# Where the stacked halves of the next attention head are copied on ScalarE: free to float, or tied behind exponentials of the current head

## The chip, the cores and the metric

The kernel runs on one core of one Trainium2 chip. A core has a matrix engine (TensorE, PE in the profile), a vector engine (VectorE, DVE), an engine for activations and copies (ScalarE, ACT), a general one (GpSimd, POOL) and DMA queues (SP issues most of them). Each engine works through its own list of instructions in order; semaphores make an instruction wait for another engine's. The metric is the device time of one execution in microseconds. Three runs of the kernel before gave 1568.66 to 1571.03 us, the median is 1570.81 us.

## What is computed

Two transformer layers over 512 image tokens and 256 context tokens, width 1024. The first layer ("even") has a gated MLP branch and a differential attention; the change touches only that attention:

```python
def diff_attn(q, k, v, lam):
    s = jnp.einsum('bqhd,bkhd->bhqk', q, k).astype(jnp.float32) * ATTN_SCALE
    p = jax.nn.softmax(s, axis=-1).reshape(b, B_HEADS, 2, tq, tk)
    a = p[:, :, 0] - lam * p[:, :, 1]
    return jnp.einsum('bhqk,bkhe->bqhe', a.astype(v.dtype), v)
```

There are four heads (B_HEADS), and each has two halves of 64 channels. Each half has a softmax of its own, and the second is subtracted from the first with the weight lam. The 512 image queries see all 768 keys, the 256 context queries only the 256 context keys.

## The kernel before

The four heads run one after the other: `head(t)` calls `attend` for three pairs of query blocks (qp 0 and 1 are image queries, qp 2 the context queries). A pair has four softmax pieces (two blocks of 128 queries, two halves c).

One softmax piece is a chain over three engines (`softmax_diff`, L534 to L545). TensorE multiplies queries and keys into a PSUM tile `pw` (L535, L536; 768 columns for image queries, 256 for context ones). There are only two such tiles, so a third piece waits until the exponential of the first has read its tile. VectorE takes the row maximum (L537), ScalarE the exponential into `e` (L539), and VectorE combines two of them (L543 to L545). Then `attend` transposes `e` on TensorE into a `pb` bank (L558); ScalarE casts the bank to `ath` and VectorE takes the rest `atl` (L131, L132); TensorE multiplies both with the values (L115 to L117, tiles `pb`), and ScalarE copies the sum into `o` (L570).

Queries and keys go in as "stacks". A product in full precision is split into a rounded part and a remainder, and 64 channels of each fill the 128 rows of the matrix engine. `stack(t, c)` (L587 to L598) builds it for half c of head t. ScalarE makes three copies of 64x768: keys into `kh` (L593), queries into `qs` (L594), keys again into the other rows of `kh` (L595). VectorE makes two subtractions of 64x768 (L596 into `qs`, L597 into `kl`). `kh` and `qs` have three buffers each: two hold the current head, one is free. So the first half of the next head can be copied as soon as its inputs are there, and the second half not before half 0 of the current head has made its last product.

`attend(t, ..., qp)` calls `stack(t + 1, 0)` at qp 1 and `stack(t + 1, 1)` at qp 2. The order of each engine's list is not the order of the code: a scheduler sets it from priorities and its own costs. `head(t)` runs at a raised priority, and ahead of it stands work that has nothing to do with the heads and can fill TensorE: `block` (projections of q and k for heads 2 and 3) and `gated` (the MLP branch). Their products are the `pf` tiles. There is one `pf` buffer, so after each of them ScalarE must copy it out (L442, L579) before the next can start. `issue_after(x)` adds an order, not a wait on another engine: what stands in its block comes behind x in the list of x's own engine.

Of the kernel before, what the change touches and what calls it, by code (L numbers as in the profile page):

```python
# [27 lines left out]
class Builder:  # L28
# [291 lines left out]
    def even(self):  # L320
        tc, nc, a = self.tc, self.nc, self.a
# [15 lines left out]
        for k in range(0, KT, 2):  # L337
            t = self.load(Rh, a["xT"][k * P:(k + 2) * P, :].rearrange("(k p) t -> p k t", p=P), [P, 2, TX], f"hx{k}")
# [111 lines left out]
        for k in range(KT):  # L450
            t = self.adap.tile([P, 2, 512], F32R, name=self.uid("wq"), tag="wq", bufs=2) if k in (2, 5) else None
# [8 lines left out]
            t, sh = hx[k], self.modcol(0, 0, k, 0)  # L460
# [31 lines left out]
        for k in range(KT):  # L492
            W = self.unit(a["v0"][k * P:(k + 1) * P, :], 512)
            for tb in range(6):
                c = slice(tb * P, (tb + 1) * P)
# [28 lines left out]
        def softmax_diff(Q, K, qb, sums):  # L524


            koff = 0 if qb < 4 else TX
            qs = slice(qb * P, (qb + 1) * P)
            nm, sums = self.small(2, "sa", 10), sums[:, 2 * qb:2 * qb + 2]
            es = []  # L530
            for c in range(2):
                ps = self.wide()
                for p in range(2):
                    if qb < 4:  # L534
                        nc.tensor.matmul(ps[:, :TX], Q[c][:, qs], K[c][p][:, :TX], start=p == 0, stop=p == 1)  # L535
                    nc.tensor.matmul(ps[:, TX:TA], Q[c][:, qs], K[c][p][:, TX:], start=p == 0, stop=p == 1)  # L536
                nc.vector.tensor_reduce(nm[:, c:c + 1], ps[:, koff:TA], axis=AX, op=ALU.max, negate=True)  # L537
                e = Ra.tile([P, TA], F32, name=self.uid("e"), tag="e", bufs=6)
                self.last_exp = nc.scalar.activation(e[:, koff:], ps[:, koff:TA], AF.Exp, bias=nm[:, c:c + 1],  # L539
                                                     accum_out=sums[:, c:c + 1])  # L540
                es.append(e[:, koff:])
            r = self.small(1, "sa", 10)
            nc.vector.reciprocal(r, sums[:, 1:2])  # L543
            nc.vector.scalar_tensor_tensor(r, r, self.nlam, sums[:, 0:1], ALU.mult, ALU.mult)
            nc.vector.scalar_tensor_tensor(es[0], es[1], r, es[0], ALU.mult, ALU.add)  # L545
            return es[0]

        def attend(t, Q, K, qp, o, eps):
            es = [softmax_diff(Q, K, 2 * qp + i, eps) for i in range(2)]
            if qp and t < 3:  # L550
                stack(t + 1, qp - 1)
            kbs = list(range(6)) if qp < 2 else [4, 5]
            po = self.bank()[:, :TC]
            for i in range(0, len(kbs), 2):
                pt = self.bank()
                for j in range(2):
                    for b in range(2):
                        nc.tensor.transpose(pt[:, j * TC + b * P:j * TC + (b + 1) * P],  # L558
                                            es[b][:, (i + j) * P:(i + j + 1) * P], self.ident)
                th = Ra.tile([P, 512], F32R, name=self.uid("ath"), tag="at", bufs=6)  # L560
                tl = Ra.tile([P, 512], F32R, name=self.uid("atl"), tag="at", bufs=6)
                self.split(th, tl, pt)
                for j in range(2):
                    kb = kbs[i + j]
                    c = slice(t * P, (t + 1) * P)
                    m = slice(j * TC, (j + 1) * TC)
                    self.mm3(po, (vhi[kb][:, c], vlo[kb][:, c]), (th[:, m], tl[:, m]),
                             i + j == 0, i + j == len(kbs) - 1)
            s = slice(qp * TC, (qp + 1) * TC)
            nc.scalar.copy(o[:, s], po)  # L570
# [13 lines left out]
            nc.gpsimd.memset(lows[i][0][64:128].bitcast(F32), 0.0)  # L584
            nc.gpsimd.memset(lows[i][1][0:64].bitcast(F32), 0.0)

        def stack(t, c):  # L587

            q, k, low = qk[t], qk[4 + t], lows[t % 2][c]
            X, Y = (slice(0, 64), slice(64, 128))[::1 - 2 * c]  # L590
            qs = Ra.tile([P, TA], F32R, name=self.uid("qs"), tag="sq", bufs=3)
            kh = Ra.tile([P, TA], F32R, name=self.uid("kh"), tag="kh", bufs=3)
            nc.scalar.copy(kh[X], k[X])  # L593
            nc.scalar.copy(qs[X], q[X])  # L594
            nc.scalar.copy(kh[Y], k[X])  # L595
            nc.vector.tensor_tensor(qs[Y], q[X], qs[X].bitcast(F32), ALU.subtract)  # L596
            nc.vector.tensor_tensor(low[X], k[X], kh[X].bitcast(F32), ALU.subtract)  # L597
            QK.setdefault(t, []).append((qs, (kh, low)))  # L598
# [51 lines left out]
        def head(t):  # L650
            Q, K = zip(*QK[t])
            o = f3("o", 4)
            eps = self.small(12, "sx", 2)
            for qp in range(3):
                attend(t, Q, K, qp, o, eps)
                if qp == 0:
                    norm(t - 1, 1)
                elif qp == 1:
                    norm(t - 1, 2)
            norms[t] = o, eps  # L660
            norm(t, 0)
            if t == 3:
                norm(t, 1)
                norm(t, 2)
            oraw.append(o)
# [50 lines left out]
        for c in range(2):  # L716
            stack(0, c)
# [42 lines left out]
        for k in order:  # L760
# [9 lines left out]
            elif k == 6:  # L770
                after = self.last_hi
# [1106 lines left out]
```

## Time and profile before

| | us |
|---|---|
| median of three runs (1568.66, 1570.81, 1571.03) | 1570.81 |
| the profiled execution, its own time | 1569.63 |
| its span | 1567.8 |
| the four heads, about | 165 to 325 |
| TensorE busy in that stretch of 160 us | 148.28 |
| VectorE busy in it | 126.38 |
| ScalarE busy in it | 98.21 |

The span runs from the first to the last instruction that the profiler saw; the time of the same execution is 1.8 us longer. "Busy" of TensorE is the time in which a matmul is in the pipeline. A row of the view of the order of time gives the start, the length, the engine, the line and, in brackets, how long the engine had been idle before and what released it.

### The profile page before, as it was taken

What the parts mean: (1) busy time and instruction counts of PE and PEld (TensorE: products, weight loads), DVE (VectorE), ACT (ScalarE), POOL (GpSimd) and SP (SyncE); (2) the same over time, 40 slices, a digit from 0 to 9 for tenths busy, and PEclk for the clock granted to TensorE, in tenths of its full rate; (3) what the DMA queues carried; (4) which work ended last, traced back from release to release, by engine and by line L of the source; (5) the groups of instructions that cost most, each with busy time, mean ns of one, the idle gap of its engine ahead of it and who ended that gap; (6) DMA issues with size and microseconds to landing.
All of it is one profiled execution on the core that took longest, in us unless ns stands there. A gap on an engine that the chain in (4) does not pass through costs nothing.

```text
span 1567.8 us, 24952 instructions
## 1 busy us (share of the span) xinstructions
PE 1513.8 (97%) x9563; PEld 1355.0 (86%) x9563; DVE 1069.2 (68%) x1890; ACT 726.4 (46%) x1489; POOL 820.0 (52%) x558
## 2 busy tenths in 40 slices
PE   6999999999999999999999999999999999999998
PEld 4767888889999999999999988777869889999997
DVE  3612777875688787888786487765657966666665
ACT  2415666563552333333333254555656544444444
POOL 0453322041256776777776454531304389888882
PEclk9999999999999999999999999999999999999999
DMA  9762100052123333454542212110224132323201
GB/s 350 298 243 74 45 21 1 1 192 77 68 76 120 114 114 116 141 160 144 168 166 70 79 55 65 57 32 16 65 106 162 55 118 91 113 90 114 89 21 55
DMA packets 53416, 162.27 MB, mean 104 GB/s; under 512 B 6192, under 2 KB 8624, under 8 KB 45616
## 3 DMA queue, kind: packets, MB, share of 16 engines
q1 hardware_dynamic: 46240, 135.37, 25.4%
q10 hardware_dynamic: 7056, 25.30, 4.9%
q8 instruction: 75, 1.23, 0.3%
q14 instruction: 45, 0.37, 0.1%
HBM read 158.55 MB, written 2.10 MB: 102 GB/s over the span
## 4 chain that ended last, share of the span: by engine, by line
PE 85%; DVE 9%; ACT 3%; issue 2%; DMA 1%; POOL 0%; DVEq 0%; SPq 0%; ACTq 0%; POOLq 0%
PE pw L116 11%; PE pw L115 11%; PE pw L117 11%; PE pb L116 9%; PE pb L115 9%; PE pb L117 9%; PE pf L115 4%; PE pf L116 4%; PE pf L117 4%; PE pb L1688 2%; PE pb L1677 2%; PE pf L359 2%; PE pw L1639 1%; PE pw L1647 1%; DVE t L49 1%
## 5 line engine op out<-in xcount | busy, mean ns | idle before, releaser
L836 DVE SCALAR_TENSOR_TENSOR xT<-pb,mod,xT 128x512 f32<-128x512 f32 (+3 forms) x204 | 143.2, 708 | 129.4 <-PE pb L117 128.9
L116 PE MATMUL pw<-ax,w 128*128 128x384 f32 (+2 forms) x716 | 227.6, 318 | 3.5 <-DVE ax L49 2.2
L115 PE MATMUL pw<-ax,w 128*128 128x384 f32 (+2 forms) x716 | 226.1, 319 | 3.6 <-DVE q L49 1.9
L117 PE MATMUL pw<-ax,w 128*128 128x384 f32 (+2 forms) x716 | 227.3, 318 | 0.1
L92 POOL TENSOR_TENSOR w<-raw,w 128x512 fp32r<-128x512 f32 (+1 forms) x76 | 111.9, 1478 | 202.0 <-ACT w L89 193.1
L49 POOL TENSOR_TENSOR w<-raw,w 128x512 fp32r<-128x512 f32 x122 | 185.1, 1533 | 48.5 <-ACT w L49 48.3
L49 POOL TENSOR_TENSOR w<-t,w 128x512 fp32r<-128x512 f32 x99 | 149.7, 1515 | 55.6 <-ACT w L49 55.6
L115 PE MATMUL pb<-hh,w 128*128 128x512 f32 x480 | 171.2, 357 | 1.2 <-DVE xT L836 1.2
L117 PE MATMUL pb<-hh,w 128*128 128x512 f32 x480 | 171.6, 357 | 0.4 <-DVE w L49 0.4
L116 PE MATMUL pb<-hh,w 128*128 128x512 f32 x480 | 171.3, 357 | 0.0
L115 PE MATMUL pw<-T,w 128*128 128x384 f32 (+1 forms) x508 | 156.6, 310 | 2.5 <-DVE hs L1044 1.2
L116 PE MATMUL pw<-T,w 128*128 128x384 f32 (+1 forms) x508 | 157.0, 310 | 1.2 <-DVE T L132 1.2
L117 PE MATMUL pw<-T,w 128*128 128x384 f32 (+1 forms) x508 | 157.0, 310 | 0.0
L115 PE MATMUL pf<-ax,w 128*128 128x256 f32 (+2 forms) x460 | 151.4, 329 | 2.1 <-DVE qf L264 1.4
L117 PE MATMUL pf<-ax,w 128*128 128x256 f32 (+2 forms) x460 | 149.3, 325 | 0.0
L116 PE MATMUL pf<-ax,w 128*128 128x256 f32 (+2 forms) x460 | 149.1, 324 | 0.0
L116 PEld LDWEIGHTS pw<-ax,w 128*128 128x128 f32 x716 | 136.4, 190 | 8.8 <-DVE ax L49 2.7
L115 PEld LDWEIGHTS pw<-ax,w 128*128 128x128 f32 x716 | 135.6, 190 | 8.0 <-DVE q L49 2.7
L117 PEld LDWEIGHTS pw<-ax,w 128*128 128x128 f32 x716 | 136.4, 190 | 2.3 <-DVE w L1007 0.4
L49 POOL TENSOR_TENSOR hh<-hs,hh 128x768 fp32r<-128x768 f32 (+1 forms) x42 | 77.3, 1839 | 95.0 <-ACT hh L49 70.9
L49 POOL TENSOR_TENSOR w<-rawo,w 128x512 fp32r<-128x512 f32 x59 | 103.6, 1756 | 28.2 <-ACT w L49 28.2
L240 DVE SCALAR_TENSOR_TENSOR junk<-ar,cb 128x1024 bf16<-128x1024 f32 x64 | 106.7, 1667 | 0.0
(417 smaller groups left out, 3909.7 us busy)
## 6 DMA issues: line engine op xcount, KB each, us to landing
raw<-ffn_in SPq DMA_DIRECT2D x44, 1024.0 KB, 5.1
ar<-ada SPq DMA_DIRECT2D x24, 1024.0 KB, 6.8
ar<-ada ACTq DMA_DIRECT2D x48, 512.0 KB, 3.6
rawo<-ffn_out SPq DMA_DIRECT2D x88, 256.0 KB, 3.0
raw<-odd_out SPq DMA_DIRECT2D x28, 256.0 KB, 2.6
raw<-qk SPq DMA_DIRECT2D x16, 256.0 KB, 4.6
raw<-uv SPq DMA_DIRECT2D x16, 256.0 KB, 2.9
raw<-even_out SPq DMA_DIRECT2D x8, 512.0 KB, 3.6
```

What stands on the lines that cost most here:

```text
L49: self.tail[key] = fn(*args, **kw)
L92: eng.tensor_tensor(lo, raw, hi.bitcast(F32), ALU.subtract)
L115: mm(out, s[0], m[0], start=start, stop=False, **kw)
L116: mm(out, s[0], m[1], start=False, stop=False, **kw)
L117: return mm(out, s[1], m[0], start=False, stop=stop, **kw)
L240: return self.nc.vector.scalar_tensor_tensor(junk, t, 1.0, self.cb[who], ALU.mult, ALU.mult, accum_out=self.acc[who][:, col:col + 1])
L359: nc.tensor.matmul(ps[32 * q:32 * q + 32, :w], cst[:, k, :], t[:, w * q:w * q + w], start=k == 0, stop=k == KT - 1, skip_group_check=True)
L836: ins = self.nc.vector.scalar_tensor_tensor(h, ps[:, r], self.modcol(l, j, m, who), h, ALU.mult, ALU.add)
L1639: nc.tensor.matmul(ps[:, st:en], Q, K[g][p][:, b0 * P:b1 * P], start=p == 0, stop=p == 1, skip_group_check=True)
L1647: last = nc.tensor.matmul(ps[:, en:en + TC], Q, K[g][p][:, TX:], start=p == 0 and not edge, stop=p == 1, skip_group_check=True)
L1677: last = nc.tensor.transpose(pt[:, x * P:(x + 1) * P], es[2 * (x % 2) + x // 2][:, kb * P:(kb + 1) * P], self.ident)
L1688: nc.tensor.matmul(po[64 * h:64 * h + 64, :], V[vb][:, 64 * g:64 * g + 64], t[:, h * TC:h * TC + TC], start=kb == 0, stop=kb == nb - 1, sk ...
```

## The change

`softmax_diff` already keeps its latest exponential in `self.last_exp`. Now `attend` also keeps the last one of qp 0 as `self.first_exps`, and `stack` gets an instruction behind which its three ScalarE copies are placed: `first_exps` for half 0 of the next head, the last exponential of qp 2 for half 1. The two VectorE subtractions are not tied. The stacks of head 0 are called without it. Nothing is added to what is computed.

```diff
         def attend(t, Q, K, qp, o, eps):
             es = [softmax_diff(Q, K, 2 * qp + i, eps) for i in range(2)]
+            if qp == 0:
+                self.first_exps = self.last_exp
             if qp and t < 3:
-                stack(t + 1, qp - 1)
+                stack(t + 1, qp - 1, self.last_exp if qp == 2 else self.first_exps)
...
-        def stack(t, c):
+        def stack(t, c, after=None):
...
-            nc.scalar.copy(kh[X], k[X])
-            nc.scalar.copy(qs[X], q[X])
-            nc.scalar.copy(kh[Y], k[X])
+            with tc.issue_after(after.ins) if after else ExitStack():
+                nc.scalar.copy(kh[X], k[X])
+                nc.scalar.copy(qs[X], q[X])
+                nc.scalar.copy(kh[Y], k[X])
```

The built programs differ in the order of all engines but the DMA queue, within the stretch of the heads. Lines behind the change are 1 to 3 higher in the new kernel. In the names below, `kh_1856` and `qs_1855` are half 1 of head 1, `kh_2177` and `qs_2176` half 0 of head 2; `e_1832` to `e_1849` are the context exponentials of head 0 (qp 2).

**ScalarE, from head 0 to head 1.** Before:

```order
L539 ACTIVATE e_1832,sx_1635<-pw_1828,sa_1821 128x256
L131 CAST ath_1699<-pb_1694 128x512
L593 CAST kh_1856<-f_58_332 64x768
L595 CAST kh_1856<-f_58_332 64x768
L131 CAST ath_1714<-pb_1709 128x512
L594 CAST qs_1855<-f_57_331 64x768
L593 CAST kh_2177<-f_219_1576 64x768
L595 CAST kh_2177<-f_219_1576 64x768
L594 CAST qs_2176<-f_211_1508 64x768
L539 ACTIVATE e_1843,sx_1635<-pw_1839,sa_1838 128x256
L539 ACTIVATE e_1849,sx_1635<-pw_1845,sa_1838 128x256
L131 CAST ath_1780<-pb_1775 128x512
```

and in the changed kernel:

```order
L539 ACTIVATE e_1832,sx_1635<-pw_1828,sa_1821 128x256
L539 ACTIVATE e_1843,sx_1635<-pw_1839,sa_1838 128x256
L131 CAST ath_1699<-pb_1694 128x512
L131 CAST ath_1714<-pb_1709 128x512
L539 ACTIVATE e_1849,sx_1635<-pw_1845,sa_1838 128x256
L596 CAST kh_1856<-f_58_332 64x768
L597 CAST qs_1855<-f_57_331 64x768
L598 CAST kh_1856<-f_58_332 64x768
L131 CAST ath_1780<-pb_1775 128x512
L572 COPY o_1634<-pb_1678 128x256
L539 ACTIVATE e_2026,sx_2018<-pw_2020,sa_2019 128x768
L442 ACTIVATE f_294_1891<-pf_1892 128x512
```

Before, six copies stand ahead of the last two exponentials of head 0. Now three stand behind the last of them, ahead of the cast `ath_1780` and of the copy that frees the one `pf` buffer.

**ScalarE, in head 1 behind its first four exponentials** (`e_2055` is the last of qp 0, `ath_1868` the cast that head 0's context queries need). The changed kernel:

```order
L539 ACTIVATE e_2047,sx_2018<-pw_2041,sa_2040 128x768
L89 CAST w_2361<-raw_2359 128x512
L539 ACTIVATE e_2055,sx_2018<-pw_2049,sa_2040 128x768
L596 CAST kh_2177<-f_219_1576 64x768
L597 CAST qs_2176<-f_211_1508 64x768
L598 CAST kh_2177<-f_219_1576 64x768
L131 CAST ath_1868<-pb_1863 128x512
L572 COPY o_1634<-pb_1774 128x256
L539 ACTIVATE e_2141,sx_2018<-pw_2135,sa_2134 128x768
```

Before, no stack copy stands between these exponentials; that half had been copied at the head's start.

**TensorE, at the same place in head 1** (`pw_2143` takes the buffer of `pw_2049`, which `e_2055` reads; `pb_1862` is the sum for head 0's context queries). The changed kernel:

```order
L535 MATMUL pw_2143<-kh_1856,qs_1855 128x512
L536 MATMUL pw_2143<-kh_1856,qs_1855 128x256
L535 MATMUL pw_2143<-kl_1044,qs_1855 128x512
L536 MATMUL pw_2143<-kl_1044,qs_1855 128x256
L115 MATMUL pb_1862<-ath_1868,vhi_1022 128x256
L560 MATMUL pb_2062<-ident_102,e_2026 128x128
L560 MATMUL pb_2062<-ident_102,e_2047 128x128
L560 MATMUL pb_2062<-ident_102,e_2026 128x128
L560 MATMUL pb_2062<-ident_102,e_2047 128x128
L535 MATMUL pw_2156<-kh_1768,qs_1767 128x512
```

The product with `ath_1868` now stands right behind the scores `pw_2143`. Before, that product came five rows ahead of `pw_2143`, behind 15 matmuls of the projection `pf_1960`; and on ScalarE `ath_1868` stood ahead of `e_2055`.

## The prediction

> **What bounds the kernel now.** I read the page first: how long the span is, who is busy, whose chain ends last.
>
> ```profile
> span 1567.8 us, 24952 instructions
> PE 1513.8 (97%) x9563; PEld 1355.0 (86%) x9563; DVE 1069.2 (68%) x1890; ACT 726.4 (46%) x1489; POOL 820.0 (52%) x558
> PE 85%; DVE 9%; ACT 3%; issue 2%; DMA 1%; POOL 0%; DVEq 0%; SPq 0%; ACTq 0%; POOLq 0%
> ```
>
> TensorE bounds it: 97% busy, 85% of the chain. The change adds no matmul, so it can act only through TensorE's idle time and its clock, and only in the heads (165 to 325 us). The second view is busy time by stretch; behind the stretch stand PE, PEld, DVE, ACT, POOL, then the granted clock.
>
> ```profile
> 180.00:200.00 20.00, 18.26 (x121) 16.33 (x120) 18.88 (x47) 11.18 (x25) 6.89 (x6) 1.00 0.11 36
> 205.00:210.00 5.00, 3.75 (x23) 2.89 (x20) 4.84 (x9) 4.87 (x7) 0.00 (x0) 0.90 0.00 0
> 210.00:215.00 5.00, 3.49 (x13) 3.06 (x13) 3.84 (x8) 3.91 (x10) 0.00 (x0) 0.50 0.00 0
> 215.00:220.00 5.00, 5.00 (x40) 4.91 (x40) 3.86 (x8) 2.33 (x6) 3.90 (x3) 0.92 0.01 3
> 220.00:240.00 20.00, 20.00 (x128) 17.91 (x127) 15.69 (x27) 13.59 (x30) 7.17 (x6) 1.00 0.04 14
> 245.00:250.00 5.00, 2.42 (x14) 1.89 (x13) 4.57 (x11) 4.90 (x11) 0.00 (x0) 0.99 0.00 0
> 250.00:255.00 5.00, 5.00 (x30) 4.81 (x29) 3.56 (x9) 2.69 (x5) 0.59 (x1) 0.67 0.00 0
> 260.00:280.00 20.00, 20.00 (x125) 17.63 (x124) 13.74 (x25) 12.96 (x26) 0.23 (x1) 1.00 0.00 1
> ```
>
> TensorE has two holes, at 205 to 215 and 245 to 250, where the next head begins. Behind each the clock falls to half for a while. The third view, the order of time on TensorE, gives the holes with their releasers; the last two rows are waits from the beginning of head 0.
>
> ```profile
> 206.38 0.39 PE L116 MATMUL pb<-atl,vhi 128*128 128x256 f32 x1 [0.53 <-DVE atl L132]
> 208.76 0.43 PE L116 MATMUL pb<-atl,vhi 128*128 128x256 f32 x1 [0.71 <-DVE atl L132]
> 211.55 0.80 PE L535 MATMUL pw<-kh,qs 128*128 128x512 f32 x1 [1.51 <-ACT e L539]
> 249.06 0.50 PE L535 MATMUL pw<-kh,qs 128*128 128x512 f32 x1 [2.58 <-ACT e L539]
> 178.10 0.50 PE L535 MATMUL pw<-kh,qs 128*128 128x512 f32 x1 [0.90 <-ACT e L539]
> 190.22 1.60 PE L699 MATMUL pb<-sq,rv 128*128 128x128 f32 x12 [1.74 <-DVE rv L700]
> ```
>
> Why the exponential is late stands on ScalarE:
>
> ```profile
> 205.44 0.83 ACT L593 CAST kh<-f 64x768 fp32r<-64x768 f32 x1
> 206.29 0.83 ACT L595 CAST kh<-f 64x768 fp32r<-64x768 f32 x1
> 207.03 0.57 ACT L131 CAST ath<-pb 128x512 fp32r<-128x512 f32 x1
> 207.63 0.83 ACT L594 CAST qs<-f 64x768 fp32r<-64x768 f32 x1
> 208.49 0.83 ACT L593 CAST kh<-f 64x768 fp32r<-64x768 f32 x1
> 209.34 0.83 ACT L595 CAST kh<-f 64x768 fp32r<-64x768 f32 x1
> 210.20 0.83 ACT L594 CAST qs<-f 64x768 fp32r<-64x768 f32 x1
> 210.94 0.47 ACT L539 ACTIVATE e<-pw,sa 128x256 f32<-128x256 f32 x1
> ```
>
> Six copies, both halves, stand ahead of it. Three alone need not hurt: at 2 to 3 they run from 276.30, and TensorE is busy 20.00 of 20.00.
>
> ```profile
> 276.30 0.83 ACT L593 CAST kh<-f 64x768 fp32r<-64x768 f32 x1
> ```
>
> **What the two holes cost.** Idle: 0.53 + 0.71 + 1.51 = 2.75 us at the first, 2.58 us at the second. Clock: work at half speed loses half its busy time, so 0.10 x 3.75 + 0.50 x 3.49 + 0.08 x 5.00 = 2.5 us, and 0.33 x 5.00 = 1.65 us. Together 5.3 and 4.2 us: 9.5 us is the most that the change can win there.
>
> **The change part by part.** The durations, from the groups of 160 to 325 us, and one row each for the spacing on TensorE (scores of 768 columns take 219.31 - 218.59 = 0.72 us):
>
> ```profile
> L539 ACT ACTIVATE e<-pw,sa 128x768 f32<-128x768 f32 x32 | 28.9, 902 | 21.1 <-DVE sa L537 19.5 <-DVE sm L620 1.5
> L539 ACT ACTIVATE e<-pw,sa 128x256 f32<-128x256 f32 x16 | 7.5, 473 | 6.6 <-DVE sa L537 6.4
> L131 ACT CAST ath<-pb 128x512 fp32r<-128x512 f32 x28 | 16.4, 585 | 8.2 <-PE pb L558 7.4 <-DVE o L648 0.5
> L593 ACT CAST kh<-f 64x768 fp32r<-64x768 f32 x6 | 5.0, 832 | 0.5 <-PE pw L536 0.4
> L570 ACT COPY o<-pb 128x256 f32<-128x256 f32 x12 | 4.5, 372 | 12.9 <-PE pb L117 12.9
> L537 DVE TENSOR_REDUCE sa<-pw 128x1 f32<-128x256 f32 x16 | 6.3, 413 | 1.7 <-PE pw L536 1.6
> L596 DVE TENSOR_TENSOR qs<-f,qs 64x768 fp32r<-64x768 f32 x6 | 5.7, 953 | 1.5 <-ACT qs L594 1.4
> 218.59 0.40 PE L535 MATMUL pw<-kh,qs 128*128 128x512 f32 x1
> 219.31 0.28 PE L116 MATMUL pb<-atl,vhi 128*128 128x256 f32 x1
> 219.43 0.28 PE L117 MATMUL pb<-ath,vlo 128*128 128x256 f32 x1
> 219.54 0.60 PE L558 MATMUL pb<-ident,e 128*128 128x128 f32 x4
> ```
>
> A product with the values takes 0.12 us (219.43 - 219.31), four transposes about 0.4. No operation is added; each of the three stacks moves by order alone, and no DMA with it. Three copies in a row are 208.49 to 211.03 at their spacing: 2.55 us. What counts is what queues behind them on ScalarE, and what TensorE still has to do meanwhile.
>
> *Head 0 to 1, half 1.* The copies come behind the last exponential, and behind them the cast `ath_1780`. From the end of the last scores `pw_1845`: maximum 0.41, exponential 0.47, copies 2.55, cast 0.59, handovers 0.1: 4.1 us. Until the product that needs the cast, TensorE has twelve products (1.4) and four transposes (0.4), 1.8 us; the next projection cannot fill in, since its `pf` buffer is freed behind the same copies. So it idles 2.3 us. Idle times of 2.58 us, and of 0.53 + 0.71, cost half clock before; I charge half of 1.65, 0.8 us. 3.1 for 5.3: **-2.2**.
>
> *Head 1 to 2, half 1.* The same chain of 4.1 us, but TensorE has some 3.2 us to do (four 512-wide matmuls of a projection at twice 0.12 each, scores 0.72, six products, eight transposes): 1.0 us, then 0.5 us for VectorE's second subtraction (0.95). 1.5 for 4.2: **-2.7**.
>
> *Half 0 of head 2.* This copy moves from a hole into a stretch that had none (220 to 240: 20.00 busy). When `e_2055` ends, TensorE may do `pw_2143` (0.72); the product behind it needs `ath_1868`, which comes 2.55 + 0.59 = 3.1 us after that exponential: 2.4 us idle. Then `pw_2156` needs `e_2141`, behind the copy into `o` (0.37 + 0.90 later): 0.7 us more, about 0.5 ahead of it all because `e_2055` itself is late. 3.6 us, and half a window of half clock, 0.8: **+4.4**. With TensorE late by itself it would be less: the ends are 1.5 and 5.5.
>
> *Half 0 of head 3.* The same place, but more work stands ahead of the scores `pw_2548`, so TensorE comes to them some 0.6 us after the exponential has ended; with their 0.72 that is 1.3 us: 3.1 - 1.3, **+1.9** (ends 1 and 3).
>
> *Half 0 of head 1.* The copies leave ScalarE ahead of head 0's first exponential and come behind its fourth. VectorE sets the pace there (18.88 of 20.00), and its work stays the same, so I expect no gain. But `pw_1747` now waits for `e_1732`, which queues behind the copies, at most 2.55 us. With the waits of 0.90 and 1.74 stretched by that I take **+1.9**.
>
> *Head 2 to 3, half 1.* The three copies that cost nothing at 276.30 now come behind the last exponential; `pw_2775` waits about 0.5 for the subtractions: **+0.5**. The end of head 3 keeps its waits, 0.
>
> Sum: -2.2 - 2.7 + 4.4 + 1.9 + 1.9 + 0.5 = +3.8 us on the profiled execution's 1569.63: 1573.4. The median of the runs is 1.2 above that execution, so 1574.6 us.
>
> The Trainium skill ("TensorE: Matmul & The Clock Gate", section "HAM oscillation — how this bites in real kernels") gives as its rule that gaps of TensorE over about 3.4 us bring the half clock. By that rule no wait of the change would, and the sum would lose its 0.8 + 0.8. The trace differs: the clock was 0.50 after 2.58 us of idling. I keep the charge; the sum without it is rival 1 below.
>
> **The rivals.**
> 1. *The clock holds.* The new idle times are 2.3 to 2.4 us, the old one that cost clock without doubt 2.58, and 1.74 at 190 cost none (1.00 from 180 to 200). Then 3.8 - 1.6 = +2.2: 1573.0, within the noise.
> 2. *Faster: the copies fit in.* Both switches become like 276.30, free: -9.5. The halves 0 cost half of their idle (1.8 + 0.9), the rest nothing: -6.8, 1564.0. For it: VectorE and ScalarE have slack (VectorE 15.69 of 20.00 from 220). Against it: the order on TensorE puts the waiting product right behind the scores. It decides if `ath_1868` ends within a microsecond of `pw_2143`.
> 3. *Every new wait halves the clock.* The two charges become full (+0.8 each) and three more places pay 1.65: +6.5, 1581.1. Against it: waits of 1.9 us and less did not do it at 190.
>
> That the copies would not stand where the change says can be left out: the order shows them there.
>
> **How the numbers follow.** Forecast 0.48, rival 1 0.20, rival 2 0.22, rival 3 0.10. What this kernel's runs can tell from no change is about 0.2%, 3.1 us: below 1567.7 faster, above 1573.9 slower. So faster 0.22, same 0.20, slower 0.48 + 0.10 = 0.58. The range leaves out half of rival 2 and half of rival 3: 1566 to 1581. The forecast's own range is 1572 to 1578.
>
> **What would show it.** Right: no three copies of `kh`, `qs`, `kh` follow on three others; TensorE idles about 2.3 us on `ath` at the first switch and 2.4 on `ath` some 15 us into head 1, the second hole shrinks to 1.5. Wrong: TensorE busy throughout head 1, with `ath` cast in time; or the holes at the switches as long as before, released by `e`. If head 1's wait is there but the time falls, the switches were worth more than I charge.

## The result and the profile after

The changed kernel takes **1574.55 us** (median of 16 runs, 1569.91 to 1578.86), the kernel before, run beside it, 1570.03 us (16 runs, 1567.87 to 1575.93). The ratio is 1.0026, with a 95% interval of 1.0017 to 1.0035: slower, by 4.5 us. The prediction said 1574.6, reckoned from the 1570.81 us that the kernel before had then.

The profiled execution of the changed kernel, from its page:

```profile
span 1572.6 us, 24957 instructions
PE 1511.5 (96%) x9563; PEld 1351.8 (86%) x9563; DVE 1071.4 (68%) x1890; ACT 725.8 (46%) x1489; POOL 820.1 (52%) x558
PE 82%; DVE 11%; ACT 3%; issue 2%; DMA 1%; POOL 0%; DVEq 0%; SPq 0%; ACTq 0%; POOLq 0%
```

TensorE's share of the chain fell from 85% to 82%: it waits more. Where, the same stretches show (behind the stretch PE, PEld, DVE, ACT, POOL, then the granted clock):

```profile
180.00:200.00 20.00, 17.00 (x113) 14.85 (x112) 19.70 (x44) 10.15 (x25) 6.58 (x5) 1.00 0.10 27
210.00:215.00 5.00, 2.83 (x19) 2.33 (x18) 4.45 (x9) 4.49 (x9) 0.00 (x0) 1.00 0.00 0
215.00:220.00 5.00, 5.00 (x42) 4.88 (x41) 5.00 (x9) 2.97 (x6) 3.07 (x3) 1.00 0.02 3
220.00:240.00 20.00, 17.81 (x116) 15.72 (x115) 14.09 (x25) 13.02 (x26) 4.42 (x4) 1.00 0.04 14
250.00:255.00 5.00, 3.50 (x18) 2.50 (x17) 4.22 (x6) 4.15 (x8) 0.00 (x0) 1.00 0.00 0
260.00:280.00 20.00, 18.58 (x128) 16.92 (x127) 14.60 (x27) 13.29 (x31) 1.30 (x1) 1.00 0.00 1
330.00:335.00 5.00, 3.27 (x12) 2.57 (x12) 5.00 (x6) 4.99 (x8) 3.30 (x3) 0.86 0.44 169
335.00:340.00 5.00, 5.00 (x25) 5.00 (x25) 5.00 (x3) 2.82 (x4) 5.00 (x3) 0.80 0.33 105
```

The two holes of before are smaller, two new ones stand at 220 to 240 and 260 to 280, and in this trace the granted clock is 1.00 behind all four. The last two rows are a place that the prediction did not look at, behind the heads, where the even output projection begins. TensorE's order of time names the releasers:

```profile
212.34 0.38 PE L115 MATMUL pb<-ath,vhi 128*128 128x256 f32 x1 [2.17 <-ACT ath L131]
224.84 0.39 PE L115 MATMUL pb<-ath,vhi 128*128 128x256 f32 x1 [1.95 <-DVE e L545]
251.34 0.39 PE L115 MATMUL pb<-ath,vhi 128*128 128x256 f32 x1 [1.14 <-ACT ath L131]
252.09 0.50 PE L535 MATMUL pw<-kh,qs 128*128 128x512 f32 x1 [0.36 <-DVE qs L599]
263.18 0.39 PE L115 MATMUL pb<-ath,vhi 128*128 128x256 f32 x1 [1.42 <-ACT ath L131]
288.70 0.47 PE L535 MATMUL pw<-kh,qs 128*128 128x512 f32 x1 [0.76 <-ACT f L581]
332.92 0.44 PE L116 MATMUL pw<-ax,w 128*128 128x384 f32 x1 [1.55 <-DVE ax L132]
```

(The row at 224.84 names VectorE's `e`, but the cast `ath` that the product reads ended at 224.79, 0.05 us ahead of it: it was `ath`.)

**The wait at 332.92** comes from a late load. On the queue of SyncE, the loads of the even output weights before:

```profile
317.38 0.81 SPq L86 DMA_DIRECT2D raw<-even_out  x2
```

and in the changed kernel (the second row begins with the second load):

```profile
313.73 0.33 SPq L86 DMA_DIRECT2D raw<-even_out  x1
320.35 0.80 SPq L86 DMA_DIRECT2D raw<-even_out  x2
```

Before, the first two went out together. Now the first goes out earlier, at 313.73, and the second only at 320.35, by the traces' own times some 2.5 us later than before. The second's staging buffer lies where head 3's buffers were, and which tile gets which buffer of a ring follows from the order of work. By the addresses in the built program, head 3's last cast `ath` lay beside that space before; now it lies in it, and the load must wait until the last products have read it (the last of them runs from 320.04, the load goes out at 320.35). ScalarE's cast of that slab and VectorE's chain follow late, and VectorE comes to run beside GpSimd. After:

```profile
324.09 1.05 ACT L89 CAST w<-raw 128x1024 fp32r<-128x1024 f32 x1 [1.56 <-DMA raw<-even_out]
327.71 2.67 DVE L630 SCALAR_TENSOR_TENSOR q<-sm,ident 128x512 f32<-128x512 f32 x2
330.30 2.57 DVE L132 TENSOR_TENSOR ax<-o,ax 128x768 fp32r<-128x768 f32 x1
328.19 3.86 POOL L132 TENSOR_TENSOR ax<-o,ax 128x768 fp32r<-128x768 f32 x2 [62.90 <-ACT ax L131]
```

The two VectorE groups took 1.02 and 0.96 us before; beside GpSimd's they take 2.67 and 2.57, and TensorE waits for the second.

**One measure for all kernels.** Each trace is cut at three instructions of ScalarE that all of them have. In the changed kernel they are:

```profile
153.61 0.62 ACT L89 CAST w<-raw 128x512 fp32r<-128x512 f32 x1 [0.89 <-PE pf L117]
320.76 0.84 ACT L643 ACTIVATE sq<-o 128x768 f32<-128x768 f32 x1
365.15 0.53 ACT L852 ACTIVATE sq<-xT 128x384 f32<-128x384 f32 x1 [13.41 <-DVE xT L839]
```

Counted from start to start: from the first to the second (head 3's squares) are the *heads*, 167.15 us; from there to the third the *handover* to the output projection, 44.39 us; from there to ScalarE's last pair of instructions the *rest*, 1201.37 us, where the order of work is the same on all five engines in the kernel before and the changed one. Before: 165.77, 42.20 and 1199.27 us.

### The profile page after: what moved, and what is told of

Read it like the earlier page. It is cut to its first block, busy times and chain, and to the rows that moved or that the text cites. A ratio compares the mean times of both kernels' runs of the same rounds, so it can differ in the third digit from the quotient of the medians.

```text
span 1572.6 us, 24957 instructions
## 1 busy us (share of the span) xinstructions
PE 1511.5 (96%) x9563; PEld 1351.8 (86%) x9563; DVE 1071.4 (68%) x1890; ACT 725.8 (46%) x1489; POOL 820.1 (52%) x558
## 4 chain that ended last, share of the span: by engine, by line
PE 82%; DVE 11%; ACT 3%; issue 2%; DMA 1%; POOL 0%; DVEq 0%; SPq 0%; ACTq 0%; POOLq 0%
PE pw L116 11%; PE pw L115 11%; PE pw L117 11%; PE pb L116 8%; PE pb L115 8%; PE pb L117 8%; PE pf L115 4%; PE pf L116 4%; PE pf L117 4%; PE pb L1691 2%; PE pb L1680 2%; PE pf L359 2%; PE pw L1642 1%; PE pw L1650 1%; DVE t L49 1%
```

## The experiments

The main question is why the moves that open the switches cost time elsewhere, and whether the terms of the prediction belong to the halves that they were put down to. Each edit is shown against the changed kernel. Ratios are to the kernel before, run beside each, with their 95% intervals.

**First: half 0 alone.**

```diff
-                stack(t + 1, qp - 1, self.last_exp if qp == 2 else self.first_exps)
+                stack(t + 1, qp - 1, None if qp == 2 else self.first_exps)
```

> Half 0 of each next stack tied as in the change, half 1 left untied as before. Theory A (each half has its own price, as in the prediction's terms): the two switches keep their holes, half 0 costs 1.9 + 4.4 + 1.9, so +8.2 us against the kernel before, about 1578. Theory B (the holes came from six copies in one pile, and moving either half away breaks the pile): at the switches three copies stand alone between exponentials, as at 276.30 in the kernel before where they cost nothing, so of the 9.5 us of the two holes nearly all is won, and half 0 gives back what its waits measured in the changed kernel's trace (1.8 + 2.2 + 1.4 = 5.4): -4 us, about 1566.

Measured: 1565.07 us, 0.9963 [0.9948, 0.9978]: faster than both kernels. Heads 160.31 us, 5.5 less than in the trace of before. Theory A is out, and the time is theory B's. B's waits are not all there: from 200 to 290 TensorE has one wait over 0.3 us left, where B had taken over some 2.2 and 1.4 us from the changed kernel (two more, 0.58 and 0.47, stand at 295 and 300):

```profile
227.08 0.50 PE L535 MATMUL pw<-kh,qs 128*128 128x512 f32 x1 [0.72 <-ACT e L539]
```

**Second: half 1 alone.**

```diff
-                stack(t + 1, qp - 1, self.last_exp if qp == 2 else self.first_exps)
+                stack(t + 1, qp - 1, self.last_exp if qp == 2 else None)
```

> Half 1 of each next stack tied as in the change, half 0 left untied as before. Theory A: the terms of half 1 alone, -2.2 - 2.7 + 0.5 = -4.4 us against the kernel before, about 1565.6. Theory B: half 0 has no reason to move, so all six copies stand in one pile behind the last exponential and ahead of the cast ath: TensorE idles 2.55 us longer at the two switches than in the changed kernel (2.2 + 2.55 = 4.7 and 1.5 + 2.55 = 4.1 us), with half clock behind each: 0 to +4 us, about 1572.

Measured: 1570.91 us, 1.0005 [0.9994, 1.0015]: the time of the kernel before. The pile behind the last exponential is there, and the first switch waits for its end:

```profile
214.05 0.80 PE L535 MATMUL pw<-kh,qs 128*128 128x512 f32 x1 [3.79 <-ACT kh L598]
```

At the second switch the pile begins here, and ends at 252.76:

```profile
247.66 1.69 ACT L596 CAST kh<-f 64x768 fp32r<-64x768 f32 x2
```

3.79 us where theory B said 4.7, but nothing at the second switch where it said 4.1: TensorE has a projection to do there and is busy 5.00 of 5.00 us both from 245 to 250 and from 250 to 255 (its one larger wait nearby, 1.21 us at 244.53, ends ahead of the pile). A pile of six does not cost the same everywhere. At the last switch, where half 1 is copied alone, waits of 1.47 on `ath` and 0.82 on the subtraction are new (288.64 and 289.85). A gain of 4.4 is excluded.

**Third: the staging buffers moved by 1248 bytes**, with nothing else changed.

```diff
+        self.slabs.tile([P, 312], F32, name=self.uid("pad"), tag="pad", bufs=1)
         self.open_ring(1024, 3, 2)
```

> The changed kernel with 1248 unused bytes ahead of the staging buffers of the even output weights, so that the second of them no longer lies on the buffer of the last cast ath of head 3 (in the kernel before it did not either). Theory: the second load starts some 3 us earlier, VectorE's subtraction and small chain end earlier, its part of the first split does not run beside GpSimd's, and the wait of 1.55 us on ax at 332.92 and the lower clock behind it go: -3.5 us against the changed kernel, about 1571. Rival (the loss at 330 to 338 is chance of this one execution, or comes from the clock alone): no change against the changed kernel, 1574.5, and the second load earlier without effect.

Measured: 1572.66 us, 1.0017 [1.0005, 1.0028]. In its trace the second load follows the first by some 1.5 us, where it was 6.6, and VectorE's rows are short again:

```profile
313.92 1.80 SPq L86 DMA_DIRECT2D raw<-even_out  x2
327.06 1.03 DVE L630 SCALAR_TENSOR_TENSOR q<-sm,ident 128x512 f32<-128x512 f32 x2
328.01 0.95 DVE L132 TENSOR_TENSOR ax<-o,ax 128x768 fp32r<-128x768 f32 x1
```

There is no wait on `ax`, and the handover takes 40.99 us instead of 44.39, with the same 167.09 us for the heads. The mechanism is confirmed in the trace, 3.4 us of it; the median fell by only half of that, 1.6 us against the control below, and the two intervals overlap.

**Fourth: the changed kernel again.**

> The changed kernel once more, as a control beside the other three and for a second trace. If the waits are set by the order: 2.2 us at the first switch, 2.0 in head 1, 1.5 at the second switch, 1.4 in head 2 and 1.5 at 333 again, within 0.2 us, and about 1574.5. If the clock is a matter of where a window falls, its low stretches (332 to 338, 983 to 993) may lie elsewhere. The other 2 us that the first trace lost at 983 to 993, where the order of work is the same in both kernels, need not come again.

Measured: 1574.28 us, 1.0029 [1.0015, 1.0043]. Heads 167.17 us, with the same waits at the switches (2.17 and 1.13 + 0.37); only the one in head 1 was 0.76 instead of 1.95, and the 1.74 at the beginning of head 0 (193.15 in the first trace) was not there; the granted clock ahead of these places was 0.71 (215 to 220) and 0.91 (180 to 200). But the handover took 42.20 us and had no wait on `ax`. The sums of squares ran at a lower clock there, and by their end the late load had been made up for:

```profile
323.06 2.35 PE L615 MATMUL pb<-ones,sq 128*128 128x128 f32 x12 [1.34 <-ACT sq L643]
329.07 1.03 DVE L630 SCALAR_TENSOR_TENSOR q<-sm,ident 128x512 f32<-128x512 f32 x2
```

**Fifth: half 0 of heads 2 and 3 alone** (head 1's as before).

```diff
-                stack(t + 1, qp - 1, self.last_exp if qp == 2 else self.first_exps)
+                stack(t + 1, qp - 1, self.first_exps if qp == 1 and t else None)
```

> As the first experiment (half 0 tied, half 1 not), but the first half 0, that of head 1, left where it was before. If the parts add up, the waits of 0.82 + 0.73 + 1.17 + 1.75 us at the beginning of head 0 go back to 0.90 + 1.74, and nothing else changes: -1.8 us against the first experiment, about 1563.3. Rival: that half 0 is what opened the first switch (it is one of the things that stood in the crowd before the end of head 0), and the hole at 206 to 212 comes back in part: 1565 to 1567.

Measured: 1564.89 us, 0.9969 [0.9955, 0.9983], heads 160.75 us. The waits at the start went back to 0.89 and 1.74, as said, but 0.53 and 1.06 came back at the first switch and 1.74 at 280.15: the rival was right that the first hole comes back in part (its time was 1565 to 1567), and the tie of head 1's half 0 costs nothing in sum.

**Sixth: half 0 four exponentials later.**

```diff
-                stack(t + 1, qp - 1, self.last_exp if qp == 2 else self.first_exps)
+                stack(t + 1, qp - 1, self.last_exp if qp == 1 else None)
```

> Half 0 tied four exponentials later, behind the last one of the second pass (qp 1), half 1 not tied. If it only matters that no six copies stand together, it is as the first experiment within 2 us: 1563 to 1567. If the place costs, the first scores of head 0 no longer wait 0.8 and 0.7 us, but the copies stand nearer to the end of the head, where each cast ath is awaited: waits of about 1 us on ath in each of three heads, 1566 to 1568.

Measured: 1574.20 us, 1.0029 [1.0018, 1.0040], heads 171.42 us. Worse than both expectations. No six copies follow on one another here, and yet it is slower: the place counts. But the threes stand close, at 192.94 and 198.57 with one exponential between them at the first switch, so the pile is loosened more than removed. The largest of the new waits, and the two subtractions of the moved half on VectorE ahead of the first of them:

```profile
201.21 0.66 PE L560 MATMUL pb<-ident,e 128*128 128x128 f32 x4 [2.68 <-DVE rv L703]
243.28 0.38 PE L536 MATMUL pw<-kh,qs 128*128 128x256 f32 x1 [1.28 <-ACT e L539]
283.59 0.38 PE L536 MATMUL pw<-kh,qs 128*128 128x256 f32 x1 [1.55 <-ACT e L539]
195.79 1.72 DVE L600 TENSOR_TENSOR kl<-f,kh 64x768 fp32r<-64x768 f32 x1
198.70 2.00 DVE L599 TENSOR_TENSOR qs<-f,qs 64x768 fp32r<-64x768 f32 x1
```

The 2.68 us end with VectorE's L703, which runs at 200.73, right behind these two (0.96 and 0.95 us each in the changed kernel at 286 to 289); the clock behind it is 0.73 (200 to 205). The other two are late exponentials. On `ath`, where about 1 us was expected, the waits are 0.40 and 0.60.

**Seventh: half 1 behind the first cast `ath`.**

```diff
                 self.split(th, tl, pt)
+                if qp == 1 and i == 0:
+                    self.first_hi = self.last_hi
...
-                stack(t + 1, qp - 1, self.last_exp if qp == 2 else self.first_exps)
+                stack(t + 1, qp - 1, self.first_hi if qp == 2 else self.first_exps)
```

> Both halves tied as in the change, but half 1 behind the first cast ath of the pass before instead of the last exponential, so that this cast no longer queues behind three copies. If ScalarE's queue ahead of ath is what made TensorE wait at the switches, the waits of 2.17 and 1.14 us on ath go and about 0.5 us on the subtraction behind the copies stays, and the even output's second load stands on buffers as in the kernel before (1.6 us, as the third experiment measured): 1570.0 to 1571.5, against 1574.3 of the changed kernel. Rival: the next waiter (the first scores of the next head, whose copies now end 0.6 us later) takes the time over: 1572.5.

Measured: 1571.20 us, 1.0006 [0.9994, 1.0018], heads 166.47 us, handover 42.20. The waits of 2.17 and 1.14 on `ath` are gone, so that queue was what TensorE waited for there. But the heads gained only 0.7 us of it: 0.56, 0.47, 0.90 and 0.93 us came in their place (212 to 238), and the 1.42 on `ath` now stands at 287. The rest of the gain in the median fits the handover, where the second load finds a free buffer here.

**Eighth: the kernel before again**, for a trace.

> The kernel before once more, for a second trace. The waits should be the same within 0.2 us (0.53, 0.71, 1.51 at the first switch, 2.58 at the second). If the half clock behind them belongs to them, it is there again, some 2.5 and 1.65 us; if it hangs on where the hole falls in time, one of the two is missing or shorter.

Measured: 1567.98 us in one run; heads 165.12, handover 42.13. The waits are the same but for one of 1.93 instead of 1.51, and the half clock is there at both holes: 0.69 in 250 to 255 (0.67 in the first trace), but at the first hole 0.71 in one stretch of 5 us where the first trace had 0.90 and 0.50. Behind 2.58 us of idling it was there both times; its length is not fixed.

**Ninth: half 1 one exponential earlier.**

```diff
+    last_exp = None
...
+                self.prev_exp = self.last_exp
                 self.last_exp = nc.scalar.activation(e[:, koff:], ps[:, koff:TA], AF.Exp, bias=nm[:, c:c + 1],
...
-                stack(t + 1, qp - 1, self.last_exp if qp == 2 else self.first_exps)
+                stack(t + 1, qp - 1, self.prev_exp if qp == 2 else self.first_exps)
```

> Both halves tied as in the change, but half 1 behind the last exponential but one instead of the last. On ScalarE's order the copies then stand one exponential later than in the first experiment (1565.1) and one earlier than in the changed kernel (1574.3). Theory C (what costs is that the copies stand behind the last exponential, where the cast ath and the next head's work queue behind them while TensorE has little left): no wait over 1 us at the switches, and the waits of 1.95 and 1.42 us in the next heads are gone too, since ScalarE is not behind there: 1564 to 1568. Rival (the price falls evenly with the place, some 9 us over two exponentials): about 1570. Rival (any tie of half 1 costs, wherever it is): 1572 to 1575.

Measured: 1565.48 us, 0.9961 [0.9948, 0.9975], heads 160.32 us. This is theory C. One exponential, at three switches, makes 6.8 us in the heads. ScalarE shows why; first the changed kernel, where the copies (209.39 to 211.81) stand behind the last exponential of head 0:

```profile
206.50 1.07 ACT L131 CAST ath<-pb 128x512 fp32r<-128x512 f32 x2 [3.25 <-PE pb L560]
208.81 0.47 ACT L539 ACTIVATE e<-pw,sa 128x256 f32<-128x256 f32 x1 [1.23 <-DVE sa L537]
209.39 0.83 ACT L596 CAST kh<-f 64x768 fp32r<-64x768 f32 x1
210.98 0.83 ACT L598 CAST kh<-f 64x768 fp32r<-64x768 f32 x1
211.72 0.57 ACT L131 CAST ath<-pb 128x512 fp32r<-128x512 f32 x1
212.58 0.90 ACT L539 ACTIVATE e<-pw,sa 128x768 f32<-128x768 f32 x1
```

and here, where they stand one exponential earlier:

```profile
204.84 0.83 ACT L598 CAST kh<-f 64x768 fp32r<-64x768 f32 x1
206.43 0.83 ACT L600 CAST kh<-f 64x768 fp32r<-64x768 f32 x1
208.08 1.07 ACT L132 CAST ath<-pb 128x512 fp32r<-128x512 f32 x2 [0.82 <-PE pb L562]
210.39 0.48 ACT L541 ACTIVATE e<-pw,sa 128x256 f32<-128x256 f32 x1 [0.73 <-DVE sa L538]
211.20 0.59 ACT L132 CAST ath<-pb 128x512 fp32r<-128x512 f32 x1 [0.25 <-PE pb L562]
212.04 0.91 ACT L541 ACTIVATE e<-pw,sa 128x768 f32<-128x768 f32 x1 [0.25 <-DVE sa L538]
```

This trace began 1.63 us later (155.24 against 153.61). With that taken off, the pair of casts starts at the same time (206.50 and 206.45) and so does the last exponential (208.81 and 208.76): the copies went into the 3.25 us that ScalarE idles for TensorE's transposes, and cost nothing. The next cast comes 2.15 us earlier (211.72 and 209.57), and with it the first exponential of the next head. The two subtractions on VectorE move along with the copies; no run holds them in place, so their share is not told apart.

**Tenth: the changed kernel a third time**, for a trace.

> The changed kernel a third time, for a trace alone. The waits at the switches as in both traces so far (2.17, 1.14 + 0.36). Open is where the clock falls: at 332 to 338 together with the wait on ax (first trace), or at 190 to 195 and 215 to 220 with no wait on ax (second). If the late load is hidden whenever the sums of squares at 322 run at a lower clock (2.35 us instead of 1.60), the third trace has either both the 1.60 and the wait, or neither.

Measured: 1577.03 us in one run. Heads 167.05, handover 44.44. Both:

```profile
323.96 1.60 PE L615 MATMUL pb<-ones,sq 128*128 128x128 f32 x12 [1.34 <-ACT sq L643]
335.28 0.44 PE L116 MATMUL pw<-ax,w 128*128 128x384 f32 x1 [1.55 <-DVE ax L132]
```

In the three traces the late load costs when the sums of squares run at full clock, in two of them.

**Eleventh: a try at a faster version.**

```diff
-            es = [softmax_diff(Q, K, 2 * qp + i, eps) for i in range(2)]
+            es = []
+            for i in range(2):
+                es.append(softmax_diff(Q, K, 2 * qp + i, eps))
+                if i == 0:
+                    self.mid_exp = self.last_exp
...
-                stack(t + 1, qp - 1, self.last_exp if qp == 2 else self.first_exps)
+                stack(t + 1, qp - 1, self.mid_exp if qp == 2 else self.first_exps if t else None)
```

> A try at a faster version: half 0 tied for heads 2 and 3 alone, half 1 tied behind the second exponential of the third pass, where ScalarE's order had it in the first experiment. If the waits at the beginning of head 0 (1.8 us) and the wait of 1.74 us at 280 in the fifth experiment both go and nothing comes back: 1562 to 1563.5. Rival: the small waits on atl and e at the first switch (0.53 and 1.06 in the fifth experiment) stay, and it is 1564.5.

Measured: 1565.72 us, 0.9958 [0.9946, 0.9970], heads 159.99 us. That is above both expectations. The 0.53 and 1.06 at the first switch stayed, as the rival said; the 1.74 at 280 went, and 0.88 and 0.69 stand at 296 and 298.

**Twelfth: the first experiment again.**

> The first experiment again, beside the two above on one chip: 1565 within 1 us, 0.9963 of the kernel before, and no hole over 1 us between 200 and 290.

Measured: 1566.49 us, 0.9961 [0.9947, 0.9975], heads 160.31 us, the same as in the first. Beside the kernel before (1571.44 in these runs) the ninth, eleventh and twelfth cannot be told apart; each is faster than the kernel before by about 0.4% and than the changed one by more.

The three pieces of each trace, in us:

| kernel | heads | handover | rest |
|---|---|---|---|
| before, two traces | 165.77, 165.12 | 42.20, 42.13 | 1199.27, 1197.19 |
| changed, three traces | 167.15, 167.17, 167.05 | 44.39, 42.20, 44.44 | 1201.37, 1201.57, 1201.64 |
| changed, staging buffers moved | 167.09 | 40.99 | 1201.55 |
| half 0 alone, two traces | 160.31, 160.31 | 43.43, 42.20 | 1200.28, 1203.06 |
| half 1 one exponential earlier | 160.32 | 41.00 | 1200.91 |
| faster try | 159.99 | 41.05 | 1201.47 |
| half 0 of heads 2 and 3 | 160.75 | 43.45 | 1203.48 |
| half 1 behind `ath` | 166.47 | 42.20 | 1202.15 |
| half 1 alone | 168.00 | 42.21 | 1198.92 |
| half 0 later | 171.42 | 41.00 | 1197.72 |

Between traces of one order the heads agree within 0.7 us. The handover takes 41.0 us at full clock without a wait; the larger values are a lower clock behind the wait for the squares, or the wait on `ax`. The rest spreads over 6 us.

## Why the prediction was right, and where its steps failed

**The total was right, but that it came within 0.1 us is luck.** The changed kernel's heads took 1.3 to 2.1 us longer than before, where the sum of the terms was +3.8. The handover, for which the prediction had 0, added 2.2 in two of three traces, and the rest, far behind the change, came out longer too. The heads alone by stretch (behind the stretch its length, then PE's busy time), before and changed:

```profile
154.34:320.11 165.77, 154.94 (x965) 136.15 (x963) 125.71 (x292) 99.73 (x211) 31.49 (x22) 0.97 0.06 19
153.61:320.76 167.15, 151.84 (x965) 132.74 (x963) 127.36 (x292) 99.49 (x211) 30.83 (x22) 1.00 0.06 19
```

TensorE idles 10.83 us before and 15.31 after, 4.5 more, and its busy time falls by 3.1, with the granted clock up from 0.97 to 1.00. The prediction's terms, taken apart in the same way, are 6.4 more idle and 2.6 of clock won. So both directions were right, and the idle was put too high.

**The waits came where the steps had them, and near their sizes**, all but one: 2.17 on `ath` at the first switch (2.3 predicted), 1.14 + 0.36 at the second (1.5), 1.42 in head 2 for half 0 of head 3 (1.9; its own 3.1 - 1.3 is 1.8), 0.76 at the last switch (0.5; the row names a copy on ScalarE that ended 0.1 us behind the subtraction which the prediction had). At the beginning of head 0 the waits grew from 2.64 to 0.81 + 0.73 + 1.17 + 1.74 = 4.45 us, +1.8 for the +1.9 predicted. The mis-sized term is half 0 of head 2: 1.95 + 0.23 in the first trace, for 3.6 of idling (2.4 + 0.7 + 0.5). The 0.5 ahead of the scores did not come, and the 0.7 behind the copy into `o` was 0.23. In the second trace the wait was 0.76; of the bounds given, 1.5 and 5.5, the lower was the nearer.

**The two clock charges failed** ("half a window of half clock, 0.8"). Behind 2.17 and 1.95 us the clock was 1.00 in the first and third trace and in that of the moved buffers; in the second it was 0.71 in 215 to 220, and the heads still took 167.17 us. TensorE was busy 154.70 us of them, 2.9 more than in the first trace, and idled 2.9 less: a lower clock ahead of a wait was taken from the wait. A charge for it on top of the wait counts it twice here. Without the charges the sum is +2.2, rival 1, and the heads' 1.3 to 2.1 are near it. The Trainium skill ("TensorE: Matmul & The Clock Gate", section "HAM oscillation — how this bites in real kernels") gives gaps over about 3.4 us as what brings half clock. On the waits of the change that was nearer than the charge in three traces of four, though both traces of before show half clock behind 2.58, and the second trace of the changed kernel 0.50 from 191 to 194, behind a wait of 1.17.

**"The end of head 3 keeps its waits, 0" failed.** The waits themselves stayed, but not the buffers: with another order the rings gave head 3's last cast another buffer, and a load behind the heads became late. The step that was missing is a look at what the loads behind the heads wait for.

**The terms do not belong to the halves.** The prediction's sum has half 1 as the gain (-4.4 with the last switch) and half 0 as the cost (+8.2). Alone, half 0 gains 4.8 to 5.5 us in the heads (against the two traces of before) and half 1 loses 2.2 to 2.9. The terms hold roughly, given that both are moved; read one by one they point the wrong way. What opens the switches is that half 0 leaves the pile; what spoils it is that half 1 goes behind the last exponential, where the first `ath` and the next head's exponentials queue. Rival 2, "the copies fit in", at 1564.0, is near what the first and the ninth experiment did (1565.07 and 1565.48).

**Open.** In the rest the changed kernel's traces are 2.1 to 4.5 us longer than those of before, at the same order of work. Part of it is one place in the later attention. In the changed kernel's first trace:

```profile
986.47 0.58 PE L1642 MATMUL pw<-kh,qb 128*128 128x256 f32 x1 [3.09 <-ACT e L1657]
```

and in the kernel before:

```profile
983.78 0.39 PE L1639 MATMUL pw<-kh,qb 128*128 128x256 f32 x1 [1.71 <-ACT e L1654]
```

The granted clock was 0.55 from 985 to 990 around the longer wait and 1.00 around the shorter. This wait has two sizes: 1.61 to 1.79 us in seven of the fourteen traces, 3.06 to 3.25 in the other seven, where the rest is longer by 2.3 us in the mean. One and the same program shows both: the changed kernel has 3.09, 1.79 and 3.25, half 0 alone 1.61 and 3.10. So the order of the copies does not settle it. In the two traces shown, ScalarE's cast of a loaded slab ahead of it (976.20 before, 978.89 in the changed kernel) waited for its load, and came 1.4 us later against TensorE's next scores (980.05 and 981.35) where the wait is long; why is not shown, and no experiment was made on it. So of the 4.5 us between the medians, some 1.3 to 2.1 are the heads and about 1.6 the late load (by the medians of the third and fourth experiment, whose intervals overlap); what is left is not attributed.

## What to carry to other kernels

Work that has a free place in an engine's queue costs by what stands behind it there: put copies for the next stage into the gap where the engine waits for others, ahead of the last instruction of the stage, not behind it; here one exponential made 6.8 us over three switches. A term that is worked out with all parts of a change in place is no price of that part: undo the parts one at a time, since half of a change that loses can win. A new order also deals ring buffers out anew, and a load into space that is reused later can become late without any line of it being touched.

## What was not expected of the hardware

Twelve matmuls of the same shape, behind the same wait of 1.33 or 1.34 us, took 1.60 us in six traces and 2.12 to 2.93 in the other eight, by the clock (1.00 from 322 to 325 in the changed kernel's first trace, 0.50 in that of before): the same wait costs clock in one execution and none in the next. A VectorE subtraction over 768 columns took 0.95 us where it began 0.36 us ahead of GpSimd's pair (third experiment), and 2.57 where it began inside the pair (first trace of the changed kernel). The Trainium skill ("SBUF — State Buffer", section "Who interferes with whom") has the two engines take turns at one pair of ports for whole instructions, when VectorE reads two operands from SBUF and GpSimd reads there too, and the trace agrees: the subtraction began at 330.30, some 0.2 us behind the start of GpSimd's second operation, and ended at 332.87, 0.8 us behind its end at 332.05, so it lost 1.6 us to what was left of one operation (3.86 / 2 = 1.9).
